# Query turns of the second head group in a list of their own, side work between the steps of norms, and the output product of eight heads inside the last attention

## The chip, the core and the metric

The kernel runs on one core of a Trainium2 chip. The metric is the device time of one execution in microseconds (us). Engines are named as in the profile: PE (TensorE, matmuls and transposes), DVE (VectorE), ACT (ScalarE), POOL (GpSimd) and SP (whose queue issues most DMAs). Every engine works through its own list of instructions in the order in which the list was written; between engines only semaphores order the work.

## The reference

Two decoder layers over x of 1024 tokens by 1024 channels, all in float32. Each layer is a token mixer and a feed-forward network, and each of these is preceded by an RMS norm with a shift and scale from a conditioning vector and followed by a gated residual sum:

```
for i in range(2):
    h = rmsnorm(x) * (1 + sc1) + sh1
    y = rglru_mixer(h) if i == 0 else dsa_mixer(h)
    x = x + g1 * y
    h = rmsnorm(x) * (1 + sc2) + sh2
    x = x + g2 * (square(relu(h @ w1)) @ w2)
```

Layer 0's mixer is a gated linear recurrence; the change does not touch that layer. Layer 1's mixer is a sparse attention: `h @ w_in` gives 16 query heads of 64, one key and value that all heads share, and 8 small indexer heads. The indexer's scores choose 256 keys for each query (a top-k by bisection); the queries attend to those alone; the 16 heads' results, 1024 channels, are multiplied by `w_out`.

## The kernel before

**Tiling.** Tokens are split into two halves (h = 0, 1) of 512, each of four blocks of 128 (t = 0 to 3 and 4 to 7). x lies with channels on partitions: eight tiles of 128 x 512 for each half. Weights come in by DMA as `raw`, are rounded by ACT into `wh` (L322) and the rest `raw - wh` goes into `wl` (L325, on POOL or DVE by the small list `self.lo`); a product is three matmuls `wh*hi`, `wh*lo`, `wl*hi` (L337 to L339).

**Order.** The Python code emits operations into a scheduler that fixes each engine's list at build time. Tiles come from pools with few slots: an instruction that needs a new tile waits until the last reader of the slot's former tile is done. Side work is held in Python generators: `self.bg` is a background whose steps `mix()` puts between main steps at `self.rate` steps each, and `self.fill` holds small steps (indexer heads, top-k) that `pump()` takes one by one.

**Layer 1 in time order.** (1) q, k, v and indexer projections of half 0, attention of half 0 (from 1378 us), its output product. (2) norm f1 of half 0 (L1396 to L1398): `stat` sums the squares by matmuls with ones (L71) and DVE and POOL take the root (L74, L76), DVE makes a diagonal (L79); `bc` broadcasts it by a matmul (L84); `apply` scales x (L102 to L104). (3) feed-forward of half 0. (4) projections and attention of half 1 (2012 to 2189 us), (5) its output product (two groups of eight heads, 96 matmuls each), (6) norm f1 of half 1, store of half 0's result, feed-forward of half 1, store of half 1.

**Queries.** `q_group` projects eight heads (group g) for four blocks, normalizes and rotates them, and appends for each block one list entry with two turns to `turns`: transposes on PE (`turn4`, L827) of two tiles that DVE and POOL write (L818, L819). A unit of attention that needs a turned query takes entries from the front of `turns` until it has its own.

**Attention.** A unit is (g, t, p): four heads of one query block; the 16 units of a half go through group 0 first. For each head: scores on PE (L1071, L1072), mask and row maximum on DVE (L1083), exponential on ACT (L1089), reciprocal of the sum on DVE (L1092), division of the whole row on POOL (L1094). Then per block of keys four heads' rows are transposed on PE (L1099), copied and rounded by ACT (L1101) and DVE (L1102), and multiplied by the values (L1111, L1112). A finished unit's result is split for the output product by ACT and POOL (L1126, 128 x 128). In half 1 the score rows `s` lie in the 13 slots that weights also use (`wh`, `wl`, `raw`). In this text heads of half 1 are counted from 0 to 63 and units from 0 to 15; unit k uses heads 4k to 4k+3, so units 8 to 15 are group 1.

The code around the change, with the order in which the parts are called:

```
self.bg, self.rate = F.f2_steps([F.NP - 2, F.NP - 1], 0), 0.8
self.attention(1, before)
self.finish()
self.reload(1)
run(self.proj_out(1, mod[1, 2], 0))
run(self.proj_out(1, mod[1, 2], 1, sqs("f1")))
```

## Time and profile before

| what | value |
|---|---|
| three runs | 2615.67, 2618.05, 2620.52 us; median 2618.05 |
| profiled execution | 2617.35 us, of which the span in the trace 2615.6 |
| PE busy | 2427.1 us, 93% of the span |
| DVE, ACT, POOL busy | 59%, 47%, 38% |
| matmuls and transposes on PE | 10834 |

The table is for the whole program. In single stages it reads differently: PE stands or runs at its lower clock for short stretches in layer 1, and in the attention of half 1 POOL has no idle time. The rows for that stand further down. In rows of the waits and of timelines "[7.28 <-POOL a L819]" means that the engine stood 7.28 us before this instruction, and that what ended last was POOL's line 819, which wrote the tile `a`. The granted clock (PEclk) is 1.00 for TensorE's upper level and 0.50 for its lower one.

### The profile page before, as it was taken

The numbers are of one execution on the slowest core, as the hardware profiler recorded it, in microseconds if no ns is written. First come the engines' busy times: TensorE is split into PE (matmuls) and PEld (weight loads), VectorE is DVE, ScalarE is ACT, GpSimd is POOL, SyncE is SP. The second block draws the span as 40 slices with busy tenths as digits, with TensorE's granted clock in tenths as the row PEclk, the third lists the DMA queues.
The fourth block names the chain that finished last, engine by engine and source line by source line (L and its number), as shares of the span: only waits on it lengthen the run. The fifth ranks groups of instructions, "written<-read, shape, count | busy, mean of one in ns | idle before, by whom it ended". The sixth has DMA issues, their size and how long they took to land. (4 is left out here: it accounts for less than half of the span.)

```text
span 2615.6 us, 30703 instructions
## 1 busy us (share of the span) xinstructions
PE 2427.1 (93%) x10834; PEld 1948.6 (74%) x10834; DVE 1546.9 (59%) x2873; ACT 1231.0 (47%) x2158; POOL 996.4 (38%) x584
## 2 busy tenths in 40 slices
PE   5689899898999999999996998999998998999999
PEld 3567678676788888888776876888887786788887
DVE  8677775579934421376686875575579894421212
ACT  3466463541122143235535767768753884433322
POOL 3454411222121244230136932223235996444342
PEclk7899999999999999999998998999999999999999
DMA  8677656326611278754431212223240003322231
GB/s 241 243 251 248 211 208 238 123 81 216 202 49 49 97 250 292 276 174 163 145 99 27 96 51 73 84 82 101 82 137 9 1 9 121 113 89 97 89 102 60
DMA packets 202748, 345.14 MB, mean 132 GB/s; under 512 B 19594, under 2 KB 109410, under 8 KB 202594
## 3 DMA queue, kind: packets, MB, share of 16 engines
q1 hardware_dynamic: 173648, 297.91, 33.6%
q10 hardware_dynamic: 28946, 45.27, 5.2%
q8 instruction: 85, 1.39, 0.2%
q14 instruction: 69, 0.57, 0.1%
HBM read 270.77 MB, written 72.35 MB: 131 GB/s over the span
## 5 line engine op out<-in xcount | busy, mean ns | idle before, releaser
L325 POOL TENSOR_TENSOR wl<-raw,wh 128x1024 fp32r<-128x1024 f32 (+2 forms) x242 | 597.1, 2476 | 1175.1 <-ACT wh L322 1128.2
L322 ACT CAST wh<-raw 128x1024 fp32r<-128x1024 f32 (+2 forms) x275 | 282.7, 1031 | 594.6 <-PE ps L338 270.7
L337 PE MATMUL ps<-a,wh 128*128 128x512 f32 x1152 | 462.5, 404 | 41.1 <-DVE a L682 13.9
L338 PE MATMUL ps<-a,wh 128*128 128x512 f32 x1152 | 461.4, 401 | 3.7 <-POOL a L664 2.2
L339 PE MATMUL ps<-a,wl 128*128 128x512 f32 x1152 | 459.4, 399 | 0.0
L337 PE MATMUL pd<-a,wh 128*128 128x512 f32 x1072 | 429.1, 401 | 21.6 <-DVE xc L595 13.8
L338 PE MATMUL pd<-a,wh 128*128 128x512 f32 x1072 | 428.0, 399 | 7.1 <-DVE a L100 5.7
L339 PE MATMUL pd<-a,wl 128*128 128x512 f32 x1072 | 427.2, 399 | 0.0
L174 DVE SCALAR_TENSOR_TENSOR a<-ps,mod,a 128x512 f32<-128x512 f32 x352 | 260.1, 745 | 264.2 <-PE ps L339 263.5
L337 PEld LDWEIGHTS ps<-a,wh 128*128 128x128 f32 x1152 | 220.0, 191 | 100.8 <-DVE a L682 16.0
L338 PEld LDWEIGHTS ps<-a,wh 128*128 128x128 f32 x1152 | 219.7, 191 | 57.9 <-POOL a L664 4.0
L339 PEld LDWEIGHTS ps<-a,wl 128*128 128x128 f32 x1152 | 219.2, 190 | 53.5
L337 PEld LDWEIGHTS pd<-a,wh 128*128 128x128 f32 x1072 | 202.4, 189 | 74.0 <-issue 14.5
L338 PEld LDWEIGHTS pd<-a,wh 128*128 128x128 f32 x1072 | 203.1, 189 | 59.8 <-DVE a L100 8.2
L339 PEld LDWEIGHTS pd<-a,wl 128*128 128x128 f32 x1072 | 203.1, 189 | 49.1
L1094 POOL TENSOR_SCALAR s<-s,rr 128x128 f32<-128x128 f32 (+7 forms) x128 | 224.9, 1789 | 22.3 <-DVE rr L1092 22.3
L337 PE MATMUL ps<-hid,wh 128*128 128x512 f32 x512 | 204.6, 400 | 12.9 <-DVE a L174 12.9
L978 ACT ACTIVATE signs<-sc,tc 128x384 int8<-128x384 f32 (+5 forms) x186 | 164.1, 882 | 92.9 <-DVE tc L993 79.4
L339 PE MATMUL ps<-hid,wl 128*128 128x512 f32 x512 | 204.0, 398 | 0.0
L338 PE MATMUL ps<-hid,wh 128*128 128x512 f32 x512 | 204.0, 398 | 0.0
L435 DVE SCALAR_TENSOR_TENSOR a<-a,cond,a 128x512 f32<-128x512 f32 x140 | 132.0, 974 | 45.0 <-DMA a<-in_ada_w_dram 44.3
L337 PEld LDWEIGHTS ps<-hid,wh 128*128 128x128 f32 x512 | 97.2, 190 | 39.4 <-DVE a L174 15.2
(270 smaller groups left out, 3715.9 us busy)
## 6 DMA issues: line engine op xcount, KB each, us to landing
raw<-in_ffn_w_dram SPq DMA_DIRECT2D x192, 512.0 KB, 3.6
a<-in_ada_w_dram ACTq DMA_DIRECT2D x160, 256.0 KB, 3.7
part<-wh SPq DMA_DIRECT2D x61, 512.0 KB, 3.6
part<-wl SPq DMA_DIRECT2D x61, 512.0 KB, 3.0
wh<-part SPq DMA_DIRECT2D x61, 512.0 KB, 3.3
wl<-part SPq DMA_DIRECT2D x61, 512.0 KB, 4.5
raw<-in_a_w_in_dram SPq DMA_DIRECT2D x20, 512.0 KB, 6.4
st<-in_ada_w_dram SPq DMA_DIRECT2D x32, 256.0 KB, 4.2
```

Of the source, the lines that this page charges most:

```text
L174: nc.vector.scalar_tensor_tensor(xt, ps, self.g2[:, m:m + 1], xt, op0=OP.mult, op1=OP.add)
L322: nc.scalar.copy(wh, raw)
L325: eng.tensor_tensor(wl, raw, wh.bitcast(FT), op=OP.subtract)
L337: pe.matmul(out, wh, xh, start=start, stop=False)
L338: pe.matmul(out, wh, xl, start=False, stop=False)
L339: pe.matmul(out, wl, xh, start=False, stop=stop)
L435: nc.vector.scalar_tensor_tensor(a, r, s, a, op0=OP.mult, op1=OP.add)
L978: A.activation(self.signs[:, 0:L], sc, AF.Sign, bias=0.0 if neg is None else neg.bitcast(FT), accum_out=n)
L1094: G.tensor_scalar(sl[e][:, 0:L], sl[e][:, 0:L], r[:, e:e + 1], None, op0=OP.mult)
```

## The change

- **Late turns.** `q_group` gets the list to append to. Group 1's entries go into `late_turns`; attention takes one entry of it after each unit from the second on, or when a unit of group 1 needs one.
- **Indexer heads in the norm of half 0.** Of the 16 head steps of blocks 6 and 7, four come ahead of `stat`, four between `stat` and `bc`, three after `apply`. The other five stay in `fill`.
- **Output product inside attention.** The first three steps of the feed-forward's background come ahead of the attention of half 1. When its rest is through and 12 units are done, x of half 1 is reloaded and group 0's output product runs in the background at 0.45 steps for each main step.
- **Stores.** Half 0's store (eight steps of four transposes, a copy and a DMA) is put around `stat` and `bc` of half 1's norm. Half of half 1's store (four steps, channels 0 to 511) is put behind the fifth to eighth output tile of the last feed-forward.

```diff
-    def q_group(self, h, g, hx):
+    def q_group(self, h, g, hx, turns):
...
-            self.turns.append([lambda p=p, turn=turn: turn(p) for p in range(2)])
+            turns.append([lambda p=p, turn=turn: turn(p) for p in range(2)])
...
+        def late():
+            for f in self.late_turns.pop(0):
+                f()
...
             while u not in self.turned:
-                if self.turns:
+                if g and self.late_turns:
+                    late()
+                elif self.turns:
                     self.turn_next()
...
             self.units = k + 1
+            if k and self.late_turns:
+                late()
             self.pump()
...
+            heads = self.idx_steps(6) + self.idx_steps(7)
+            some(4)
             N["f1", 0].stat()
+            some(4)
             N["f1", 0].bc()
             hf[0] = N["f1", 0].apply(mod[1, 4], mod[1, 3])
-            for t in (6, 7):
-                self.fill += self.idx_steps(t) + [lambda t=t: self.fill.extend(self.topk_steps(t))]
+            some(3)
+            self.fill += heads + self.topk_steps(6) + self.topk_steps(7)
...
-            self.bg, self.rate = F.f2_steps([F.NP - 2, F.NP - 1], 0), 0.8
+            f2 = F.f2_steps([F.NP - 2, F.NP - 1], 0)
+            for _ in range(3):
+                next(f2)
+            def background():
+                yield from f2
+                while self.units < 12:
+                    yield
+                self.reload(1)
+                self.rate = 0.45
+                yield from self.proj_out(1, mod[1, 2], 0)
+            self.bg, self.rate = background(), 0.8
             self.attention(1, before)
             self.finish()
-            self.reload(1)
-            run(self.proj_out(1, mod[1, 2], 0))
             run(self.proj_out(1, mod[1, 2], 1, sqs("f1")))
+            out0 = self.store(0, 0)
+            out0 += self.store(0, 1)
+            for f in out0[:3]:
+                f()
             N["f1", 1].stat()
+            for f in out0[3:6]:
+                f()
             N["f1", 1].bc()
             hf[1] = N["f1", 1].apply(mod[1, 4], mod[1, 3])
-            self.store(0)
-            FFN(self, 1, mod[1, 5], hf).single(1)
-            self.store(1)
+            for f in out0[6:]:
+                f()
+            early = self.store(1, 0)
+            def last(h, m):
+                if m >= 4:
+                    early.pop(0)()
+            FFN(self, 1, mod[1, 5], hf, last).single(1)
+            for f in self.store(1, 1):
+                f()
```

Three places in the engines' lists, of before and of the change. The first is PE's list at the start of half 0's attention: `ps<-identR,a` are the turns (L827), `ps<-ident,s` the transposes of score rows, `wh` and `wl` with 128 x 328 the key and value projection. Before:

```order
5300 L1072 MATMUL ps_11055<-a_8197,a_10235 128x384
5301 L827 MATMUL ps_11097<-identR,a_10782 128x128 x4
5302 L827 MATMUL ps_11103<-identR,a_10785 128x128 x4
5303 L827 MATMUL ps_11109<-identR,a_10796 128x128 x4
5304 L827 MATMUL ps_11115<-identR,a_10799 128x128 x4
5305 L827 MATMUL ps_11121<-identR,a_10810 128x128 x4
5306 L827 MATMUL ps_11127<-identR,a_10813 128x128 x4
5307 L1099 MATMUL ps_11133<-ident,s_10857 128x128 x4
5308 L778 MATMUL ps_11142<-wh_10887,a_10609 128x328
```

The same place in the changed kernel:

```order
5301 L1105 MATMUL ps_11097<-ident,s_10857 128x128 x4
5302 L778 MATMUL ps_11106<-wh_10887,a_10609 128x328
5303 L779 MATMUL ps_11106<-wl_10888,a_10609 128x328
5304 L780 MATMUL ps_11106<-wh_10887,a_10610 128x328
5305 L1105 MATMUL ps_11110<-ident,s_10940 128x128 x4
5306 L778 MATMUL ps_11106<-wh_10887,a_10627 128x328
5307 L779 MATMUL ps_11106<-wl_10888,a_10627 128x328
5308 L780 MATMUL ps_11106<-wh_10887,a_10628 128x328
5309 L827 MATMUL ps_11122<-identR,a_10782 128x128 x4
```

Six groups of four turns stood in front of the first score transposes; now these and six projection matmuls come first, the first two groups follow among the projection, and the other four later.

The second place is DVE's list at norm f1 of half 0, where `sc<-ir,wi,sc` (L954) adds an indexer head to the scores, L63 adds a square to the norm's sum, and L74, L79 and L102 belong to `stat` and `apply`. Before:

```order
1757 L63 TENSOR_TENSOR nl_12729<-nl_12729,ns_13063 128x512
1758 L954 SCALAR_TENSOR_TENSOR sc_12888<-ir_13070,wi,sc_12888 128x512
1759 L954 SCALAR_TENSOR_TENSOR sc_12888<-ir_13075,wi,sc_12888 128x256
1760 L74 TENSOR_SCALAR rs_13086<-ps_13081 128x4
1761 L991 TENSOR_SCALAR tl_13214<-tn_13215 128x1
1762 L993 TENSOR_SCALAR tc_13218<-tl_13214,tc_13060 128x1
1763 L79 TENSOR_SCALAR nl_13090<-ident,rs_13088 128x128 x4
1764 L991 TENSOR_SCALAR tl_13220<-tn_13221 128x1
```

In the changed kernel:

```order
1757 L63 TENSOR_TENSOR nl_12729<-nl_12729,ns_13063 128x512
1758 L993 TENSOR_SCALAR tc_13060<-tl_13056,tc_13036 128x1
1759 L954 SCALAR_TENSOR_TENSOR sc_12888<-ir_13070,wi,sc_12888 128x512
1760 L954 SCALAR_TENSOR_TENSOR sc_12888<-ir_13075,wi,sc_12888 128x256
1761 L950 TENSOR_SCALAR sc_13081<-ps_13083,wi 128x384
1762 L954 SCALAR_TENSOR_TENSOR sc_13081<-ir_13094,wi,sc_13081 128x512
1763 L954 SCALAR_TENSOR_TENSOR sc_13081<-ir_13099,wi,sc_13081 128x384
1764 L954 SCALAR_TENSOR_TENSOR sc_13081<-ir_13106,wi,sc_13081 128x512
1765 L954 SCALAR_TENSOR_TENSOR sc_13081<-ir_13111,wi,sc_13081 128x384
1766 L954 SCALAR_TENSOR_TENSOR sc_13081<-ir_13118,wi,sc_13081 128x512
1767 L954 SCALAR_TENSOR_TENSOR sc_13081<-ir_13123,wi,sc_13081 128x384
1768 L74 TENSOR_SCALAR rs_13131<-ps_13126 128x4
```

Between the last L63 and L74 stand now four heads' adds more, and seven adds between L79 and the first L102.

The third place is POOL's list in the last quarter of half 1's attention, where 128 x 1024 and 128 x 896 with `s<-s,rr` are the divisions of one head each. Before:

```order
476 L1094 TENSOR_SCALAR s_18811<-s_18811,rr_18815 128x1024
477 L1094 TENSOR_SCALAR s_18847<-s_18847,rr_18851 128x1024
478 L1094 TENSOR_SCALAR s_18882<-s_18882,rr_18886 128x1024
479 L1094 TENSOR_SCALAR s_18917<-s_18917,rr_18921 128x1024
480 L1094 TENSOR_SCALAR s_18944<-s_18944,rr_18948 128x1024
481 L325 TENSOR_TENSOR wl_19244<-raw_19241,wh_19243 128x1024
482 L1094 TENSOR_SCALAR s_18980<-s_18980,rr_18984 128x1024
```

In the changed kernel, from head 56 on:

```order
470 L1100 TENSOR_SCALAR s_18742<-s_18742,rr_18746 128x1024
471 L325 TENSOR_TENSOR wl_18788<-raw_18785,wh_18787 128x1024
472 L1132 TENSOR_TENSOR a_16956<-a_18673,a_16955 128x128
473 L1132 TENSOR_TENSOR a_16958<-a_18673,a_16957 128x128
474 L1132 TENSOR_TENSOR a_16960<-a_18673,a_16959 128x128
475 L1132 TENSOR_TENSOR a_16962<-a_18673,a_16961 128x128
476 L325 TENSOR_TENSOR wl_18794<-raw_18791,wh_18793 128x1024
477 L1100 TENSOR_SCALAR s_18809<-s_18809,rr_18813 128x1024
478 L1100 TENSOR_SCALAR s_18846<-s_18846,rr_18850 128x1024
479 L1100 TENSOR_SCALAR s_18893<-s_18893,rr_18897 128x1024
480 L1100 TENSOR_SCALAR s_18934<-s_18934,rr_18938 128x1024
481 L1100 TENSOR_SCALAR s_18977<-s_18977,rr_18981 128x1024
```

Another `wl` and then the last two divisions follow, so three splits of weights stand ahead of the last head's division where one stood. PE's list there, in unit 12, has the first matmuls of the output product between transposes of this unit's score rows:

```order
8546 L337 MATMUL ps_18797<-a_16947,wh_18787 128x512
8547 L338 MATMUL ps_18797<-a_16948,wh_18787 128x512
8548 L1105 MATMUL ps_18819<-ident,s_18491 128x128
8549 L1105 MATMUL ps_18819<-ident,s_18526 128x128
8550 L1105 MATMUL ps_18819<-ident,s_18560 128x128
8551 L1105 MATMUL ps_18819<-ident,s_18596 128x128
8552 L1105 MATMUL ps_18856<-ident,s_18491 128x128
8553 L339 MATMUL ps_18797<-a_16947,wl_18788 128x512
8554 L337 MATMUL ps_18797<-a_16949,wh_18787 128x512
```

Row 8553 reads the `wl` that POOL writes in its row 471; before, these matmuls stood behind the whole attention.

## Rows read from the trace of the kernel before

**Rows 1.** The engines over the whole span, from the page.

```profile
PE 2427.1 (93%) x10834; PEld 1948.6 (74%) x10834; DVE 1546.9 (59%) x2873; ACT 1231.0 (47%) x2158; POOL 996.4 (38%) x584
```

**Rows 2.** What PE waited for from 1370 us: total, times, longest, us.

```profile
PE ps L827 <- POOL a L819: 13.9, 5, 7.3
PE ps L1099 <- POOL s L1094: 11.2, 7, 4.3
PE ps L71 <- DVE nl L63: 8.9, 2, 6.2
```

**Rows 3.** PE's timeline, start of half 0's attention: start, length, instruction, idle before.

```profile
1387.50 0.34 PE L1072 MATMUL ps<-a,a 128*128 128x384 f32 x1
1395.11 0.75 PE L827 MATMUL ps<-identR,a 128*128 128x128 f32 x4 [7.28 <-POOL a L819]
```

**Rows 4.** Windows: length; busy (count) of PE, PEld, DVE, ACT, POOL; clock; DMA.

```profile
1390.00:1400.00 10.00, 2.25 (x12) 1.69 (x12) 10.00 (x31) 3.11 (x10) 9.52 (x10) 0.57 0.00 0
1400.00:1410.00 10.00, 4.58 (x21) 3.88 (x22) 4.24 (x14) 1.29 (x3) 9.06 (x11) 0.50 0.20 45
```

**Rows 5.** DVE's timeline in the same stretch.

```profile
1402.28 0.87 DVE L766 TENSOR_TENSOR q<-q,a 128x512 f32<-128x512 f32 x1
1407.73 0.69 DVE L1102 TENSOR_TENSOR pl<-ps,nl 128x512 fp32r<-128x512 f32 x1 [4.58 <-ACT nl L1101]
```

**Rows 6.** PE's timeline at norm f1 of half 0.

```profile
1575.08 1.87 PE L71 MATMUL ps<-ones,nl 128*128 128x1 f32 x8 [6.18 <-DVE nl L63]
1581.40 2.05 PE L84 MATMUL ps<-nl,ones 128*128 128x512 f32 x2 [4.45 <-DVE tl L991]
```

**Rows 7.** DVE's timeline there.

```profile
1578.31 2.94 DVE L79 TENSOR_SCALAR nl<-ident,rs 128x128 f32<-128x128 f32 x4 [0.85 <-POOL rs L76]
1583.48 2.06 DVE L102 SCALAR_TENSOR_TENSOR ns<-a,mod,ps 128x512 f32<-128x512 f32 x3 [1.92 <-PE ps L84]
```

**Rows 8.** Lines by shape, DVE, 1380 to 2010: an indexer head's adds.

```profile
L954 DVE SCALAR_TENSOR_TENSOR sc<-ir,wi,sc 128x512 f32<-128x512 f32 x35 | 30.8, 899 | 6.0 <-ACT ir L953 5.7
L954 DVE SCALAR_TENSOR_TENSOR sc<-ir,wi,sc 128x384 f32<-128x384 f32 x7 | 4.3, 610 | 0.0
```

**Rows 9.** Windows in half 1's attention and the product after it.

```profile
2120.00:2140.00 20.00, 19.49 (x116) 15.88 (x116) 18.23 (x40) 18.36 (x39) 20.00 (x13) 1.00 0.00 1
2160.00:2180.00 20.00, 12.75 (x63) 9.75 (x62) 7.96 (x15) 10.17 (x19) 20.00 (x12) 0.83 0.23 79
2180.00:2200.00 20.00, 19.95 (x93) 15.50 (x92) 9.65 (x14) 10.11 (x19) 11.21 (x9) 0.92 0.59 210
2200.00:2220.00 20.00, 20.00 (x88) 16.05 (x87) 5.95 (x8) 4.45 (x6) 9.54 (x4) 1.00 0.34 106
```

**Rows 10.** POOL's timeline, heads 51 to 63.

```profile
2139.20 18.27 POOL L1094 TENSOR_SCALAR s<-s,rr 128x896 f32<-128x896 f32 x7
2157.35 1.81 POOL L1126 TENSOR_TENSOR a<-a,a 128x128 fp32r<-128x128 f32 x4
2159.05 14.23 POOL L1094 TENSOR_SCALAR s<-s,rr 128x1024 f32<-128x1024 f32 x5
2173.15 2.44 POOL L325 TENSOR_TENSOR wl<-raw,wh 128x1024 fp32r<-128x1024 f32 x1
2175.48 2.94 POOL L1094 TENSOR_SCALAR s<-s,rr 128x1024 f32<-128x1024 f32 x1
```

**Rows 11.** PE's timeline: unit 15's start, last product, norm of half 1.

```profile
2178.47 0.47 PE L1099 MATMUL ps<-ident,s 128*128 128x128 f32 x1 [4.33 <-POOL s L1094]
...
2233.74 0.40 PE L339 MATMUL ps<-a,wl 128*128 128x512 f32 x1
2236.83 1.05 PE L71 MATMUL ps<-ones,nl 128*128 128x1 f32 x8 [2.69 <-DVE nl L63]
```

**Rows 12.** Timeline of all engines, end of the program.

```profile
2606.06 3.85 PE L1193 MATMUL ps<-ident,a 128*128 128x128 f32 x32
```

**Rows 13.** DMA issues, from the page: count, KB, us from issue to landing.

```profile
raw<-in_ffn_w_dram SPq DMA_DIRECT2D x192, 512.0 KB, 3.6
```

More of the change, by code (lines that the diff above doesn't have):

```diff
@@ L1185, in reload, with store, step @@
             self.nc.sync.dma_start(self.x[h, m], self.xd[h, m])
-    def store(self, h):
+    def store(self, h, c):
         nc = self.nc
-        for t in range(4):
-            for c in range(2):
-                ps = self.ps()
-                for b in range(4):
-                    nc.tensor.transpose(ps[:, b * P:(b + 1) * P], self.x[h, 4 * c + b][:, t * P:(t + 1) * P],
-                                        self.ident)
-                o = self.tmp("o")
-                (nc.scalar.copy if (t + c) % 2 else nc.vector.tensor_copy)(o, ps)
-                r = h * 4 + t
-                (nc.scalar if h == 0 else nc.sync).dma_start(
-                    self.out[0, r * P:(r + 1) * P, c * 512:(c + 1) * 512], o)
+        def step(t):
+            ps = self.ps()
+            for b in range(4):
+                nc.tensor.transpose(ps[:, b * P:(b + 1) * P], self.x[h, 4 * c + b][:, t * P:(t + 1) * P], self.ident)
+            o = self.tmp("o")
+            (nc.scalar.copy if (t + c) % 2 else nc.vector.tensor_copy)(o, ps)
+            r = h * 4 + t
+            (nc.scalar if h == 0 else nc.sync).dma_start(self.out[0, r * P:(r + 1) * P, c * 512:(c + 1) * 512], o)
+        return [lambda t=t: step(t) for t in range(4)]
     def run(self):
@@ L1241, in flush @@
                 turn_next()
-        self.turns, self.turn_next, self.turned = turns, turn_next, set()
+        self.turns, self.turn_next, self.turned, self.late_turns = turns, turn_next, set(), []
         NJ = 8
@@ L1339, in run @@
                       lambda: (idx(2), idx(3)), lambda: None, lambda: None, lambda: None,
-                      lambda: (flush(), run(self.q_group(0, 0, hm[0])))]
+                      lambda: (flush(), run(self.q_group(0, 0, hm[0], turns)))]
             for p in range(NJ, F.NP):
@@ L1354, in run @@
             self.lo = [1, 1, 0]
-            q1 = self.q_group(0, 1, hm[0])
+            q1 = self.q_group(0, 1, hm[0], self.late_turns)
             hm[1] = []
@@ L1391, in run, with some @@
                 heads.pop(0)()
+            heads = self.idx_steps(6) + self.idx_steps(7)
+            def some(n):
+                for _ in range(n):
+                    heads.pop(0)()
+            some(4)
             N["f1", 0].stat()
+            some(4)
             N["f1", 0].bc()
             hf[0] = N["f1", 0].apply(mod[1, 4], mod[1, 3])
-            for t in (6, 7):
-                self.fill += self.idx_steps(t) + [lambda t=t: self.fill.extend(self.topk_steps(t))]
+            some(3)
+            self.fill += heads + self.topk_steps(6) + self.topk_steps(7)
             self.lo, self.npump = [1, 1, 0], 2
@@ L1403, in run @@
             self.lo = [1, 0]
-            run(self.q_group(1, 0, hm[2]))
-            run(self.q_group(1, 1, hm[2]))
+            run(self.q_group(1, 0, hm[2], turns))
+            run(self.q_group(1, 1, hm[2], self.late_turns))
             self.lo = [1]
```

## The prediction, made before the changed kernel ran

> **What bounds the kernel now.** I read the page's engine line, then the view of waits for PE over layer 1, then windows and timelines of the four places that the diff names. The engine line says that PE is busy 93% of the span [rows 1]; the change takes no matmul away, so all it can win is PE's idle time and time at the lower clock, and only where PE's next work is not held by another engine. The view of waits names the holders from 1370 us: turns that wait for POOL's rotation (13.9 us), score transposes that wait for POOL's division (11.2) and the two norms' sums that wait for DVE (8.9) [rows 2]. The reader is to see that these three lie in three stages with different limits.
>
> At the start of half 0's attention PE ends its scores at 1387.50 and stands until 1395.11 for the first turn [rows 3]; in the next 20 us it works 2.25 and 4.58 us, at a granted clock of 0.57 and 0.50, while DVE is full until 1400 and POOL until 1410 [rows 4]. In half 1's attention POOL works 20.00 us of 20 [rows 9]: the divisions of the heads follow one another without a gap, and PE is in step with them. Unit 15's first transpose starts at 2178.47, after 4.33 us of waiting for POOL [rows 11], and POOL's last division began at 2175.48 [rows 10]. After the attention it is the other way round: PE 20.00 of 20, POOL 9.54 [rows 9].
>
> **Late turns in half 0: −8 us.** Six groups of turns leave the place ahead of the first score transposes. Two of the six (block 0 of group 1) come soon after and still wait for POOL until 1395, but now 8 transposes and 6 projection matmuls are done by then, and the rest of the 24 projection matmuls between and behind them. What is late next is DVE: its list up to the rotation that starts at 1402.28 and takes 0.87 is the same in both kernels, and the first rounding of transposed scores (L1102) stands behind it. There DVE idles 4.58 us before, since ACT's copy, and PE's transposes, stand behind the turns [rows 5]; now the roundings can run at 1403.2. The first costs 4.58 less. Behind it DVE works 4.39 of the ten us to 1420, so about as much again can be won until DVE's and POOL's own work (9 us of 10 in POOL's windows until 1410) closes in: 3 us at least, 14 at most (PE's idle time in 1390 to 1410, 7.75 + 5.42 = 13.2, and something for the clock), and I take 8, nearer to what DVE shows. The four groups that go on to later units are 16 transposes, under 2 us, which were executed before as well.
>
> **Heads in the norm of half 0: −2.5 us.** PE stands 6.18 us before `stat` and 4.45 before `bc` [rows 6]. Eleven heads are 44 matmuls; eight heads with two of 512 columns (0.23 us each, 20.00 for 88 [rows 9]) and two of 384 (0.17 by columns), three with four of 512, are 8 x 0.80 + 3 x 0.92 = 9.2 us of PE work that leaves the feed-forward behind. Against it: in DVE's list four heads' adds stand between the last square and L74. Their first is one instruction of 0.6 us, the others 3 x (0.90 + 0.61) = 4.5 [rows 8], so the root, the diagonal and `bc` come 5 us later. Between the diagonal and the first scaling stand seven adds, 3 x 0.90 + 4 x 0.61 = 5.1 us, of which the 2.2 us from the diagonal's end (1581.25) to 1583.48 are covered [rows 7]: 2.9 late. The scaling starts some 7 to 8 us later than at 1583.48 and PE's feed-forward with it; 9.2 less 7 is 2.2, and a little of the lower clock is gained. Ends: +2 if the lower clock stays as long as the longer wait, −8 if the heads' adds hide between DVE's other work. I take −2.5.
>
> **Stores: −2.5 us together.** At half 1's norm 24 transposes in place of standing time save 24 x 3.85 / 32 = 2.9 us [rows 12]; two copies on DVE stand ahead of the last square, 0.7 us lost: −2. At the end 16 transposes in place of 32 and four copies fewer save about 2.3 us, but the other 16 now stand in the feed-forward, where PE has no idle time, and cost 1.9: −0.5. The DMAs are issued from the lists of ACT and SP as before. Ends −4 and 0.
>
> **Output product of group 0 in the attention: +11 us.** The intent: 96 matmuls of 0.23 us, 22 us, go to where PE waits. What there is to fill: in 2160 to 2180 PE idles 7.25 us, and at clocks of 0.83 and 0.92 it loses 0.17 x 12.75 + 0.08 x 19.95 = 3.8 in the two windows [rows 9]: 11 us, the end of the range on this side (the stretches before have 0 to 2.5 of 20, in small pieces).
>
> But the product brings its weights' split along, and it stands in POOL's list, on the engine that is full. I count from the end of head 51's division, t0. Seven heads take 2139.20 to 2157.35; with four more of the first five's kind it is 5 x 2.50 + 2 x 2.82, so t0 = 2141.7, when unit 12 starts. Four splits of results take 1.7, a head of 1024 columns 2.82, a `wl` 2.33 (2173.15 to 2175.48) [rows 10].
> - POOL now: heads 52 to 55, 10.0; head 56, to 12.8; first `wl`, to 15.2.
> - PE now: two matmuls with `wh` and five transposes into unit 12 it meets the first matmul with `wl`. It gets there at about 4.4, when the weights' load (3.6 us [rows 13]), issued near the end of unit 11, and ACT's rounding are through, and stands until 15.2: **10.8 us, with the rest of unit 12 behind it**. In the kernel before PE did not stand there.
> - POOL next: the second `wl` waits for its load, which takes the place of the first one's `raw`, and for a slot that unit 12's transposes free: about 26. The `s` tiles of heads 57 and 58 need such slots too: head 57 from 28, heads 58 and 59 to 36.5. Heads 60 and 61 take the slots of the first `wh` and `wl`, whose last reader is late in unit 13: 42.7 to 48.3; third `wl` 50.7, heads 62 and 63 to 56.3. Before, head 63 ended at 36.6 (2175.48 + 2.82 − 2141.7).
> - PE to the end: unit 12 ends at 28, unit 13 at 43, unit 14 waits some 3 us for the third `wl`, unit 15 2 us for the fourth; with 89 matmuls of the product inside, the attention ends near 77. The other 103, at 0.23, end at 101, and 2 us for the lower clock behind the 10.8 us make 103. Before, the last matmul ended at 2234.1 [rows 11], at 92.4.
>
> The difference is 10.6; I take +11. It is +3 if POOL comes to the first `wl` a few heads earlier than its place says, and +20 if each of the four `wl` holds PE as the first one does. The three steps of the feed-forward ahead of the attention fill waits of PE before it, but POOL's chain starts when DVE's rotations are done, and those keep their order: 0, between −2 and +1.
>
> On this a page bears. In these rows one stage is full on POOL and the next on PE. The Trainium skill, "Perfetto Trace Analysis", section "Optimization Strategy", says that where the most-contended engine changes over time, interleaving such regimes may help. By it the term would be −11 instead of +11. I don't follow it, since the row of `wl` shows that the piece moved is not of PE alone.
>
> **The sum.** −8 − 2.5 − 2.5 + 11 = −2 against the profiled 2617.35 us (span 2615.6 and 1.75 around it). The median of the runs is 0.7 above that, so 2616. A measurement of this kernel can't tell a change within 0.2% (5.2 us) from none.
>
> **Rivals.**
> 1. *The product fills PE's waits.* POOL comes to the first `wl` in time, or PE's standing there is covered. For it: 11 us of losses at the end of the attention, and a POOL with 9.54 of 20 behind it. Against: the row in POOL's list behind head 56. Price: −8 − 2.5 − 2.5 − 11 = −24, so 2594; half of it, with a term of 0, 2605.
> 2. *Slower: the lower clock behind the stall.* After the 7.28 us of standing at 1387 the clock was 0.50 to 0.57 for 20 us [rows 3, 4], with little work in them; unit 12 to 14 are dense work. A matmul costs double at the lower of the two levels; 20 us of it do 10 us of full work. Price +10 on the sum, so 2626, and with further stands for `wl` 2631. It decides from some 7 us of loss by the clock on. The Trainium skill, "TensorE: Matmul & The Clock Gate", "Part 1: The HAM clock gate", says that the throttled state is the default and activity releases it; that rule is for this rival, and by it the time is the one given here.
> 3. *Late turns win nothing.* POOL works 9.52 and 9.06 of 10 until 1410 [rows 4], and what it does there is the same; if the divisions of the next units wait behind its rotations, PE only waits elsewhere. Price: 8 us back, 2624.
> 4. *It doesn't do what it says.* The background might not reach the product before the units are over; then the term is 0: 2605. The list shows 89 matmuls inside, which speaks against it.
>
> **How the numbers follow.** My forecast, 2612 to 2623 when the parts cancel: 0.34. Rival 1 with its half and rival 4: 0.37, nearly all faster. Rival 2: 0.19. Rival 3 and the like: 0.10. So faster 0.37, no difference 0.34, slower 0.29. The range leaves out the full price of rival 1 and the far end of rival 2: 2598 to 2632; the forecast's own is 2611 to 2623.
>
> **What would show it.** In the new trace: PE standing about 11 us in unit 12 before L339, released by POOL's L325; POOL with two gaps of some 6 us in the attention's last quarter; the last division 15 to 20 us later against unit 12's start; PE's wait at 1387 down from 7.28 to pieces; `stat` of half 0 with heads before it and L74 5 us later. Wrong I am if PE's idle time in the attention's last quarter shrinks, or if 1387 to 1424 loses as much as before.

## The result and the profile after

The changed kernel takes 2630.66 us (median of 5 runs, 2627.64 to 2634.67) against 2618.05 for the kernel before on the same chip. The ratio is 1.0051, with a 95% interval of 1.0039 to 1.0064: 12.6 us slower. The forecast was 2616, no difference, from a sum of -2 over the steps of the change.

To find where the time went I cut both traces at the same instructions and compared how long each piece took. The pieces come from single profiled executions; the stretch ahead of the first piece (layer 0 and the first projections), which the change leaves as it was, differs by 2.6 us between the two, so a piece under some 2 us is not read as a gain or a loss by itself. The profiled execution of the changed kernel took 2634.42 us, 3.8 above its median. All pieces run from the start of one instruction to the start of the next one named.

| piece | before, us | change, us | forecast |
|---|---|---|---|
| first scores of half 0 to `stat` (attention, its product) | 195.5 | -1.8 | late turns -8 |
| `stat` to first matmul of the feed-forward | 9.9 | +6.1 | heads: +7 |
| that to the last projection matmul of half 1 | 395.9 | -11.1 | heads: -9.2 |
| that to the first score transpose of half 1 | 41.7 | +4.2 | three steps: 0 |
| that to the division of head 51 | 116.6 | +0.5 | 0 |
| that to the division of head 63 | 36.3 | +22.5 | product: |
| that to the last matmul of the product | 58.2 | -4.6 | +11 with the row above |
| from there to the end | 381.9 | -1.3 | stores: -2.5 |

The engines over the whole span, to be held against [rows 1]: PE's busy time is up by 13.3 us with the same 10834 instructions. A matmul that runs at the lower clock is busy for longer (the fence on unit 12 below has 0.80 us for one that takes 0.40 elsewhere). Most of it is no work of the change: 8.3 us lie ahead of half 0's attention, where PE is busy 1260.9 us before and 1269.3 now for the same 5390 instructions.

```profile
PE 2440.4 (93%) x10834; PEld 1958.1 (74%) x10834; DVE 1531.6 (58%) x2873; ACT 1231.3 (47%) x2158; POOL 995.3 (38%) x584
```

What PE waited for from 1370 us on (total, times, longest, us), to be held against [rows 2]:

```profile
PE ps L339 <- POOL wl L325: 13.8, 4, 9.0
PE ps L827 <- DVE a L174: 10.9, 1, 10.9
PE ps L1105 <- POOL s L1100: 7.6, 8, 2.2
PE ps L778 <- DVE mn L1089: 5.7, 1, 5.7
PE ps L1077 <- DVE mn L1089: 5.3, 2, 3.1
PE ps L1105 <- DVE pl L1108: 4.2, 3, 2.2
PE ps L84 <- DVE nl L79: 4.1, 2, 2.6
```

Of the three leaders of before only the divisions are left (7.6 us for 11.2); the turns' wait for POOL and the norms' wait for L63 have shrunk to 0.3 and 1.4 us. In their places stand two new releasers with 24.7 us together, a weight split on POOL and an addition on DVE (L174). Both belong to what was moved into or ahead of half 1's attention.

**The product inside the attention.** POOL's timeline from head 49 on; 128 x 1024 and 128 x 896 on L1100 are divisions of a head, L325 the splits of weights. Before, it was a chain without a gap [rows 10].

```profile
2137.19 17.88 POOL L1100 TENSOR_SCALAR s<-s,rr 128x896 f32<-128x896 f32 x7
2155.00 2.37 POOL L325 TENSOR_TENSOR wl<-raw,wh 128x1024 fp32r<-128x1024 f32 x1
...
2168.04 2.37 POOL L325 TENSOR_TENSOR wl<-raw,wh 128x1024 fp32r<-128x1024 f32 x1 [9.01 <-PE ps L1105]
2172.69 8.49 POOL L1100 TENSOR_SCALAR s<-s,rr 128x1024 f32<-128x1024 f32 x3 [2.28 <-PE pd L1078]
2187.68 5.67 POOL L1100 TENSOR_SCALAR s<-s,rr 128x1024 f32<-128x1024 f32 x2 [6.51 <-DVE rr L1098]
2193.32 2.35 POOL L325 TENSOR_TENSOR wl<-raw,wh 128x1024 fp32r<-128x1024 f32 x1
2195.66 5.66 POOL L1100 TENSOR_SCALAR s<-s,rr 128x1024 f32<-128x1024 f32 x2
```

The engine that had no idle time now stands 9.01, 2.28 and 6.51 us. PE's timeline in unit 12 says why, and then the end of the product:

```profile
2147.10 0.50 PE L337 MATMUL ps<-a,wh 128*128 128x512 f32 x1 [1.74 <-ACT wh L322]
...
2147.67 0.71 PE L1105 MATMUL ps<-ident,s 128*128 128x128 f32 x5
2157.42 0.80 PE L339 MATMUL ps<-a,wl 128*128 128x512 f32 x1 [9.05 <-POOL wl L325]
...
2227.36 0.80 PE L338 MATMUL ps<-a,wh 128*128 128x512 f32 x1 [2.76 <-POOL a L1132]
```

PE stands until POOL, behind heads 52 to 56, has made the first `wl`; POOL then stands until PE, late by that, has released slots for the second one (its wait of 9.01 us ends with a transpose of score rows, L1105). Each waits for the other in turn. The windows show it for both, and what the clock did (columns as in [rows 4], to be held against [rows 9]):

```profile
2140.50:2160.50 20.00, 7.42 (x29) 5.64 (x30) 3.75 (x8) 5.48 (x13) 18.52 (x11) 0.77 0.14 49
2160.50:2180.50 20.00, 18.18 (x90) 14.00 (x89) 11.40 (x20) 9.88 (x17) 10.19 (x4) 0.97 0.08 28
2180.50:2200.50 20.00, 16.02 (x77) 12.29 (x77) 12.29 (x23) 12.08 (x24) 13.49 (x6) 0.91 0.16 53
```

One window over the whole stretch, from the end of head 51's division to the product's last matmul, tells how much of the loss is standing and how much is the clock. First before, then changed:

```profile
2141.80:2234.15 92.35, 85.03 (x404) 67.33 (x402) 49.34 (x82) 47.98 (x84) 64.46 (x36) 0.94 0.31 103
2142.24:2252.50 110.26, 88.67 (x403) 69.02 (x404) 48.54 (x78) 48.31 (x83) 64.17 (x37) 0.91 0.19 63
```

PE stands 21.6 us in place of 7.3, which is 14.3 of the 17.9 us; its busy time for the same matmuls is 3.6 us longer, at a mean granted clock of 0.91 in place of 0.94.

**The start of half 1's attention.** PE's timeline, and then DVE's of the same moment:

```profile
1985.58 0.40 PE L339 MATMUL ps<-a,wl 128*128 128x512 f32 x1
1996.92 1.23 PE L827 MATMUL ps<-identR,a 128*128 128x128 f32 x8 [10.94 <-DVE a L174]
```

```profile
1995.43 0.69 DVE L766 TENSOR_TENSOR q<-q,a 128x512 f32<-128x512 f32 x1
1996.03 0.75 DVE L174 SCALAR_TENSOR_TENSOR a<-ps,mod,a 128x512 f32<-128x512 f32 x1
1996.69 0.49 DVE L818 CAST a<-q 128x256 fp32r<-128x256 f32 x2
```

The three early steps of the feed-forward run on PE until 1985.6. A matmul's result lies in a bank of PSUM, and the bank can be written anew when another engine has read it. The banks that the three steps filled are emptied by L174, and in DVE's list the last of these stands among the rotations of queries. The next turn needs a bank, so it waits 10.94 us for a DVE instruction that is in no hurry. Before, PE's larger waits in this place were two, of 6.6 us together:

```profile
1986.01 1.26 PE L827 MATMUL ps<-identR,a 128*128 128x128 f32 x8 [4.26 <-ACT q L908]
...
2000.36 0.50 PE L337 MATMUL ps<-a,wh 128*128 128x512 f32 x1 [2.37 <-DVE a L174]
```

**The norm of half 0.** PE, DVE and POOL, to be held against [rows 6, 7]:

```profile
1575.90 1.70 PE L71 MATMUL ps<-ones,nl 128*128 128x1 f32 x8
1585.33 2.04 PE L84 MATMUL ps<-nl,ones 128*128 128x512 f32 x2 [2.55 <-DVE nl L79]
```

```profile
1580.21 0.15 DVE L74 TENSOR_SCALAR rs<-ps 128x4 f32<-128x4 f32 x1
1584.31 0.88 DVE L79 TENSOR_SCALAR nl<-ident,rs 128x128 f32<-128x128 f32 x4 [3.29 <-POOL rs L76]
1589.20 2.06 DVE L102 SCALAR_TENSOR_TENSOR ns<-a,mod,ps 128x512 f32<-128x512 f32 x3
```

```profile
1580.32 2.96 POOL L325 TENSOR_TENSOR wl<-raw,wh 128x1024 fp32r<-128x1024 f32 x1 [3.75 <-ACT wh L322]
1583.24 1.04 POOL L76 TENSOR_TENSOR rs<-rs,mhalf 128x4 f32<-128x4 f32 x1
```

The wait before `stat` is gone and the one before `bc` is 2.55 instead of 4.45. The scaling starts 13.3 us after `stat` where it took 8.4 before. Of the 4.9 us that this is later, 2.4 are the heads' adds ahead of L74 (4.3 us after `stat`; it was 1.9). From L74 to the diagonal it is 2.8 us longer, and that is on POOL: the root (L76) now stands behind a split of weights, 2.96 us long, that began 0.11 us after L74. The rest nearly cancels: the diagonal is done in 0.88 us where it took 2.94 [rows 7], and the seven adds behind it put the scaling off by 1.8.

**Late turns.** PE at the start of half 0's attention, then the windows, 2.6 us later than those of [rows 4] because the attention starts so much later; then DVE:

```profile
1390.30 0.60 PE L1105 MATMUL ps<-ident,s 128*128 128x128 f32 x4
1396.55 0.64 PE L778 MATMUL ps<-wh,a 128*128 128x328 f32 x1 [5.65 <-DVE mn L1089]
```

```profile
1392.60:1402.60 10.00, 6.05 (x31) 5.41 (x32) 10.00 (x31) 3.59 (x11) 9.52 (x10) 0.66 0.00 0
1402.60:1412.60 10.00, 6.43 (x31) 4.80 (x29) 8.69 (x27) 3.87 (x13) 10.00 (x13) 0.74 0.24 53
1412.60:1422.60 10.00, 5.92 (x19) 4.63 (x19) 4.93 (x17) 4.20 (x10) 5.59 (x8) 0.50 0.00 1
```

```profile
1404.94 0.87 DVE L766 TENSOR_TENSOR q<-q,a 128x512 f32<-128x512 f32 x1
1405.73 0.68 DVE L1108 TENSOR_TENSOR pl<-ps,nl 128x512 fp32r<-128x512 f32 x1
...
1415.78 0.26 DVE L856 TENSOR_SCALAR kk<-kk,ss 128x64 f32<-128x64 f32 x1 [2.91 <-POOL ss L855]
```

DVE's hole of 4.58 us [rows 5] is filled, the rounding follows the last rotation at once, as forecast. But the wait of 7.28 us [rows 3] is only moved: the first matmul of the projection stands 5.65 us, now for a bank that DVE's row maximum (L1089) has to read first, and that stands in DVE's list behind rotations. And the third window, in which PE did 33 matmuls at a clock of 0.84 before, has 19 at 0.50.

**Stores.** The last transposes, against [rows 12]: a run of 20 is left, and the program ends 2.3 us sooner after the feed-forward's last matmul.

```profile
2625.48 2.54 PE L1202 MATMUL ps<-ident,a 128*128 128x128 f32 x20
```

### The profile page after: what moved, and what is told of

Same layout as the page of the kernel before. It is cut to its first block, busy times and chain, and to the rows that moved or that the text cites. A ratio compares the mean times of both kernels' runs of the same rounds, so it can differ in the third digit from the quotient of the medians.

```text
span 2632.6 us, 30717 instructions
## 1 busy us (share of the span) xinstructions
PE 2440.4 (93%) x10834; PEld 1958.1 (74%) x10834; DVE 1531.6 (58%) x2873; ACT 1231.3 (47%) x2158; POOL 995.3 (38%) x584
## 5 line engine op out<-in xcount | busy, mean ns | idle before, releaser
L325 POOL TENSOR_TENSOR wl<-raw,wh 128x1024 fp32r<-128x1024 f32 (+2 forms) x242 | 596.9, 2474 | 1183.3 <-ACT wh L322 1141.2
L174 DVE SCALAR_TENSOR_TENSOR a<-ps,mod,a 128x512 f32<-128x512 f32 x352 | 260.5, 747 | 271.8 <-PE ps L339 271.0
L339 PEld LDWEIGHTS ps<-a,wl 128*128 128x128 f32 x1152 | 219.8, 191 | 68.5 <-POOL wl L325 15.2
L337 PEld LDWEIGHTS pd<-a,wh 128*128 128x128 f32 x1072 | 203.3, 190 | 72.4 <-issue 13.3
L1100 POOL TENSOR_SCALAR s<-s,rr 128x128 f32<-128x128 f32 (+7 forms) x128 | 225.0, 1777 | 34.9 <-DVE rr L1098 31.7
L152 DVE TENSOR_TENSOR a<-r,a 128x512 fp32r<-128x512 f32 x64 | 47.3, 761 | 139.4 <-ACT a L151 138.1
```

The costliest lines, as they stand in the source:

```text
L152: nc.any.tensor_tensor(ql, r, qh.bitcast(FT), op=OP.subtract)
L174: nc.vector.scalar_tensor_tensor(xt, ps, self.g2[:, m:m + 1], xt, op0=OP.mult, op1=OP.add)
L325: eng.tensor_tensor(wl, raw, wh.bitcast(FT), op=OP.subtract)
L337: pe.matmul(out, wh, xh, start=start, stop=False)
L339: pe.matmul(out, wl, xh, start=False, stop=stop)
L1100: G.tensor_scalar(sl[e][:, 0:L], sl[e][:, 0:L], r[:, e:e + 1], None, op0=OP.mult)
```

## The experiments

The kernel before ran again in each batch (medians 2618.0 to 2621.8), so I compare ratios to it; 0.001 is 2.6 us.

**Which of the two pieces at half 1 costs.** Without the product inside, without the three steps, and without either:

```diff
# e1_no_product (and e3)
-                while self.units < 12:
-                    yield
-                self.reload(1)
-                self.rate = 0.45
-                yield from self.proj_out(1, mod[1, 2], 0)
...
+            self.reload(1)
+            run(self.proj_out(1, mod[1, 2], 0))
# e2_no_three (and e3)
-            for _ in range(3):
-                next(f2)
```

> The changed kernel with group 0's output product put back behind the attention of half 1; all else as changed. Theory P (the product inside the attention costs 17 to 18 us, because its weights' splits stand in POOL's full list and hold PE): 2630.7 less 17.6, about 2613. Rival F (the three feed-forward steps ahead of the attention are the main cost, by the 11 us for which PE then waits for DVE): the product's removal gives little, about 2627.

> The changed kernel without the three feed-forward steps ahead of the attention of half 1; the product stays inside. Theory P: the three steps cost only the 4.2 us of lead that PE has at the last query projection and has lost when the first score transposes start, so about 2626.5, and PE's stand of 9 us in unit 12 stays. Rival F: about 2619.

> The changed kernel with both undone: the product behind the attention and no feed-forward steps ahead of it. Left are late turns, indexer heads and stores. If the parts add up: 2630.7 - 17.6 - 4.2 = 2609, that is 9 us faster than before. If late turns in half 1 also cost something, 2612 to 2616.

Measured: e1 2613.57, ratio 0.9984 (0.9975 to 0.9993); e2 2627.79, 1.0036 (1.0023 to 1.0050); e3 2608.20, 0.9963 (0.9951 to 0.9976). All three came as expected, within 1.5 us. In e1 the piece with heads 51 to 63 is 36.3 us long again, in e2 the piece before the first transpose is as before. So the product inside costs some 18 us (e3 to e2: 0.0073 x 2620 = 19) and the three steps some 5 (0.0021 x 2620 = 5.5); the rest of the change wins 9.7.

**What in the product costs.** Two suspects: POOL's split of the weights, and the slots that score rows and weights share. All these kernels are without the three early steps, except e4. In e4 and e12 DVE makes `wl` (from there on, so that of group 1's product too). In e5 and e6 the weights of half 1's product of group 0 stand in half-size tiles of another pool, so that a split of 128 x 1024 becomes two of 128 x 512, and group 1's weights are still split by POOL. So a row and a column of the table below differ by a little more than their heading says.

```diff
# e4_wl_dve, e12_dve_shared_slots
                 self.rate = 0.45
+                self.lo = [0]
# e5_own_slots_pool; in e6_own_slots_dve nc.vector in place of nc.gpsimd
+            raw = self.wp.tile([P, 2, 512], FT, name=self.nm("raw"), tag="raw", bufs=3)
+            self.nc.sync.dma_start(raw, src)
+            for e in range(2):
+                wh, wl = self.tileR(), self.tileR()
+                self.nc.scalar.copy(wh, raw[:, e])
+                self.nc.gpsimd.tensor_tensor(wl, raw[:, e], wh.bitcast(FT), op=OP.subtract)
```

> The changed kernel with the product's weights split by DVE in place of POOL. Theory P1 (their place in POOL's list is the cost): PE's stand of 9 us for the first one goes, POOL loses four splits (9.4 us), the last division comes some 10 us earlier against unit 12's start; 2616 to 2620. Rival P2 (slots: the product's weights take six of the 13 slots that score rows need, so divisions wait for transposes, whoever splits): POOL's two gaps of 9.0 and 6.5 us before heads 57 and 60 stay, PE's stand only moves; 2626 to 2630.

> As e2 (product inside the attention, no early feed-forward steps), but the product's wh and wl lie in eight tiles of the activations' pool, so that only raw takes slots of the score rows; POOL still splits. Theory P1 (POOL's list) : PE's stand of 7 to 9 us in unit 12 stays, the gaps of POOL before heads 57 and 60 shrink, in all 3 to 6 us less than e2's 2627.8: 2622 to 2625. Theory P2 (slots): both gaps go and with them most of the loss, 2612 to 2616.

> As e5, with DVE as the splitter. If place in POOL's list and slots were the whole of what kept the product from filling PE's waits, it should now give what the page's rule promises: up to 11 us less than e3's 2608.2, so 2598 to 2604. If PE had nothing to win there (its waits are given back to the unit that comes later), 2607 to 2612. DVE works 18 of 20 us there, so it may become the holder: 2612 to 2616.

> e6 with the product's weights back in the 13 slots that they share with score rows, DVE as the splitter (that is e4 without the early feed-forward steps). If slots and splitter are two separate costs: e4's 2615.5 less 4, 2611, that is 7 us more than e6. If DVE's splitting alone is what counts, 2604 to 2606.

| ratio to before | split on POOL | split on DVE |
|---|---|---|
| shared slots | e2 1.0036 (1.0023 to 1.0050) | e12 0.9965 (0.9953 to 0.9977) |
| own slots | e5 1.0002 (0.9994 to 1.0011) | e6 0.9944 (0.9931 to 0.9958) |
| product not inside | e3 0.9963 (0.9951 to 0.9976) | |

e4 gave 2615.50 (0.9992, 0.9981 to 1.0002), e5 2620.66, e6 2604.12, e12 2612.79. e5 lies between the two theories; e4 and e6 lie at the edge of the first range that each named, and e12, 5.5 us behind e6 by the ratios, is nearer to two separate costs than to one. Splitting on DVE is worth 18.6 us with shared slots and 15 with own ones; own slots 9 and 5.5. The traces have the same order: from the end of head 51's division to the product's last matmul it is 92.3 us before, 110.0 in e2, 102.5 in e5, 95.5 in e12 and 85.1 in e6. Both costs are real, POOL's list is the larger. POOL's timeline in e4 shows the second one alone: no split is left on it, and it still stands twice (in e12, which has no early steps, 7.87 and 5.66 us).

```profile
2132.08 17.89 POOL L1100 TENSOR_SCALAR s<-s,rr 128x896 f32<-128x896 f32 x7
...
2159.24 8.49 POOL L1100 TENSOR_SCALAR s<-s,rr 128x1024 f32<-128x1024 f32 x3 [7.60 <-DVE rr L1098]
2173.41 12.38 POOL L1100 TENSOR_SCALAR s<-s,rr 128x1024 f32<-128x1024 f32 x4 [5.68 <-DVE rr L1098]
```

In e6 neither is left. POOL divides to the end without a gap, and PE's windows show the product in what were its waits:

```profile
2133.08 18.47 POOL L1100 TENSOR_SCALAR s<-s,rr 128x896 f32<-128x896 f32 x7
...
2151.88 2.93 POOL L1100 TENSOR_SCALAR s<-s,rr 128x1024 f32<-128x1024 f32 x1
...
2155.98 17.06 POOL L1100 TENSOR_SCALAR s<-s,rr 128x1024 f32<-128x1024 f32 x6
```

```profile
2154.50:2174.50 20.00, 19.70 (x109) 16.01 (x107) 17.22 (x30) 13.01 (x24) 18.54 (x10) 1.00 0.24 80
2174.50:2194.50 20.00, 19.51 (x110) 15.91 (x110) 12.22 (x20) 12.19 (x24) 8.82 (x7) 1.00 0.41 132
```

PE works 19.70 and 19.51 us of 20 at a granted clock of 1.00, where [rows 9] had 12.75 at 0.83. From the division of head 51 to the last matmul of the product it is 7.2 us less than before: in the trace a gain of the kind that rival 1 spoke of is there, but not to be had with this weight path. e6 is faster than both kernels, by 15 us against before. Against e3, which leaves the product outside, it is 5 us by the ratios, and the two intervals still overlap, so that the product inside wins anything at all rests on the trace.

**The parts alone**, each put into the kernel before:

```diff
# e7_late_only (cut)
-            q1 = self.q_group(0, 1, hm[0])
+            q1 = self.q_group(0, 1, hm[0], self.late_turns)
...
+            if k and self.late_turns:
+                late()
...
# e8_heads_only (cut)
+            some(4)
             N["f1", 0].stat()
+            some(4)
             N["f1", 0].bc()
...
# e11_stores_only (cut)
-            self.store(0)
...
+            out0 = self.store(0, 0)
...
```

> The kernel before with late turns alone, in both halves. The forecast's term was -8: 2610. The two traces show 2 to 3 us from 1378 us to the norm's statistics of half 0 and nothing at the first transposes of half 1: 2615 to 2616.

> The kernel before with the indexer heads between the norm's steps alone. The forecast's term was -2.5: 2615.5. The two traces show 4 to 5 us between the norm's statistics of half 0 and the query projection of half 1: 2613 to 2614.

> The kernel before with the stores moved alone. The forecast's term was -2.5; the stages of the traces so far give -1.2 from the norm of half 1 to the feed-forward, +1.3 within it and -2.3 at the end: 2618 less 2.2, 2616. If the parts' sum (e3, -9.8) lacks 5 us that late turns and heads alone don't show, they must be here: 2612.

Measured: e7 2617.96, 0.9993 (0.9984 to 1.0001); e8 2618.38, 0.9997 (0.9986 to 1.0008); e11 2619.18, 0.9993 (0.9982 to 1.0003). Each interval reaches to no change. By the ratios e7 and e11 are 1.8 us faster, in line with what was expected of the traces, and e8 0.8, where 4 to 5 were expected: a miss. Together the three win 0.0017 of the time, and e3, which has all three, wins 0.0037 (0.0024 to 0.0049): 5 us apart. In the traces the heads' pieces are in e8 as in e3 (+6.2 and -11.1), with 1.2 us lost in the piece before them, where four heads run ahead of `stat`; and late turns win 3.0 in half 0 in e7, so the -1.8 of the changed kernel is -3.0 and these +1.2; but the piece from head 63 to the end of the product is 1.0 to 1.7 us longer than before in each of the three, and 0.2 shorter in e3. Why is open; the margins of the four ratios allow most of it to be noise.

**Why late turns won 1.8 and not 8.** First the place of group 1's rotations: e9 (on e3) and e10 (on e6) put them behind the projection of keys and values inside the attention, e13 (on e3) ahead of it.

```diff
# e9_late_rotation, e10_best (e13_rotation_first: `yield from q1` as the first line of the background)
-            run(q1)
             self.drain()
...
                 yield from feed(self.kv_steps(1, hm[1]), 2)
+                yield from q1
```

> e3 (no product inside, no early feed-forward steps), and group 1's rotations of half 0 are done in the attention's background behind the projections of the second half's keys, not ahead of the attention. Theory R (late turns won 2 to 3 us in place of 8 because group 1's rotations still stand ahead on DVE and POOL: score reductions, and with them PE's banks, wait behind them): PE's stand of 5.6 us for DVE's reduction goes, half 0's norm starts 5 to 10 us earlier than e3's, 2598 to 2603. Rival S (POOL's divisions bind half 0's attention later on anyway): no earlier norm, 2607 to 2610.

> e6 (product inside, its weights in tiles of their own, split by DVE) with the late rotations of e9. If the two add up, e6's 2604.1 less what e9 gains on e3: 2594 to 2599 by theory R, 2603 to 2606 by rival S.

> The changed kernel without the product inside and without the three early steps (2608), and in the background of half 0's attention the rotations of group 1 stand first, ahead of the projection's roundings and norms. If the late turns won 1.8 us and not 8 because score roundings on DVE stand behind group 1's rotations at places that hold PE's PSUM banks (5.65 and 3.09 us of standing), then these stands go or move together and half 0's attention is some 5 us shorter: 2603. If POOL's list sets the stretch (its share of the rotations and the key norm's L855 at 1415.8 behind them), nothing changes: 2608.

Measured: e9 2630.41, 1.0032 (1.0021 to 1.0044); e10 2623.34, 1.0005 (0.9993 to 1.0017); e13 2622.56, 1.0002 (0.9993 to 1.0012). All three miss, on the slow side. In e9 the wait of 5.6 us is gone, and the largest waits of PE between 1375 and 1590 are now at the first units of group 1, which reach rotations that are late:

```profile
PE ps L1077 <- DVE mn L1089: 12.4, 2, 8.5
PE ps L827 <- POOL a L819: 9.8, 1, 9.8
```

Half 0's attention is 9.7 us longer than in e3, and half 1's 6.3 us (12.9 lost behind its first transpose, 6.6 won before it); that second loss I did not follow up. In e13 half 0 is 1.6 us longer and half 1 7.6. So the rotations are not simply in the way where they stand: moved either way, they cost more.

Then POOL's share: in e14 (on e3) ACT divides the score rows of the first two blocks, for the heads of group 0.

```diff
# e14_act_divides
-                G.tensor_scalar(sl[e][:, 0:L], sl[e][:, 0:L], r[:, e:e + 1], None, op0=OP.mult)
+                if t < 2 and g == 0:
+                    A.activation(sl[e][:, 0:L], sl[e][:, 0:L], AF.Copy, scale=r[:, e:e + 1])
+                else:
+                    G.tensor_scalar(sl[e][:, 0:L], sl[e][:, 0:L], r[:, e:e + 1], None, op0=OP.mult)
```

> The same kernel (2608) with the divisions of the first two blocks' scores in half 0's attention on ACT in place of POOL. If POOL's list sets the first 40 us of the attention, the key norm of group 1 (L856, at 1415.8) comes some 7 us earlier and half 0's attention ends some 5 us earlier: 2603. If DVE's list and the PSUM banks set it, L856 comes earlier but the attention's length stays: 2608. A loss of some us is possible if ACT, which copies and rounds in the same stretch, is then late for PE.

Measured: 2614.03, 0.9969 (0.9959 to 0.9980), no different from e3 (0.9963). The windows:

```profile
1390.00:1400.00 10.00, 3.56 (x20) 3.06 (x19) 10.00 (x31) 7.68 (x28) 2.53 (x3) 0.72 0.07 25
1400.00:1410.00 10.00, 8.96 (x46) 7.62 (x45) 9.52 (x32) 6.03 (x18) 6.23 (x7) 0.77 0.20 45
```

POOL works 2.53 and 6.23 of ten where it had nearly all, and DVE is as full as in the changed kernel (10.00 and 9.52 here, 10.00 and 8.69 there). The key norm (L856) comes 31.8 us after the attention's start instead of 33.6 in e3, and half 0's attention is 1.6 us shorter, while POOL has nearly 11 us less to do in these two windows. ACT took the work over (7.68 and 6.03 us of ten), so a loss there that hides a gain is not excluded, but ACT is not full. With that reservation the theory that POOL's list sets this stretch falls. DVE's list remains, nearly full for these 20 us in the changed kernel and in e14. No run made it shorter: that it is the limit is what is left over, not what was shown.

## Why the prediction was wrong

**The product inside: right mechanism, +17.9 where I had taken +11.** PE stood where it was said to and for what: 9.05 us plus 1.74 for `wh`, the first `wl` at +15.2 us after head 51's end, as worked out; the second `wl` at 25.8 against "about 26". From there POOL ran 2.3 to 2.8 us late (head 57 started at 30.5 and not 28, head 63 ended at 59.1 and not 56.3), and the attention on PE ended at 79.3, not 77. Behind the attention 103 matmuls took 30.6 us, not 24 + 2. There PE stands once more, 0.94 us for ACT and 2.76 us for POOL, which makes three weight splits (7.04 us) ahead of the last unit's results, and the next 13 matmuls start 0.43 us apart, at a clock of 0.66 in the windows there, instead of 0.23. The step that failed here is the end of the walk: the forecast followed POOL's list to the last division and not to its next consumer. The far end of the term, +20, held the result, but by luck: it was to come if each `wl` held PE as the first did, and the other three held it 4.8 us together.

**The three steps: 0, between -2 and +1, was wrong; +4.2 by the trace, 3.9 to 7.1 by the runs.** This is the step whose reason failed. I said that POOL's chain starts when DVE's rotations are done and those keep their order. They do, but PE's work ahead of the attention has another end on DVE: L174, which empties its PSUM bank. It stands among the rotations, and the turn behind it stood 10.94 us. The steps filled a wait of PE and made a longer one. That I costed them by PE and POOL alone, without asking who releases the bank, is the mistake. Three pairs of kernels show the cost: e1 against e3 5.5 us, the full change against e2 3.9, e4 against e12 7.1.

**Late turns: -8 was too much; -1.8, or -3.0 alone.** The filled hole in DVE's list was right, and what it was said to be worth "at least", 3 us, is what came. I took 8 as "nearer to what DVE shows". The step that failed is "8 transposes and 6 projection matmuls are done by then": by 1397.6, the same moment 2.6 us later, it was 4 and 3, because the first projection matmul stood 5.65 us for a bank that DVE frees behind rotations. It is the same omission as with the three steps. What closed in is named in the prediction, DVE's and POOL's own work, but its date was wrong: it closes in at once. PE did more in the two first windows (6.05 and 6.43 us against 2.25 and 4.58 [rows 4]), at granted clocks of 0.66 and 0.74, and then stood again. What would win the rest of the 8 us stays open. That this is rival 3's case, nearly, is true in size. Its reason (POOL) is not: e14 took most of POOL's work away and won 1.6.

**Heads: -5.0 where I had -2.5; -3.8 with the 1.2 us ahead of `stat` (e8).** Eleven heads took 11.1 us out of the feed-forward, not 9.2, and the start came 6.1 us later against some 7. The delay has another make-up than I worked out: 2.8 us of it are POOL's weight split ahead of the root. In the times it shows less than in the trace (e8).

**Stores: -1.3 in the full change, -2.2 without the three steps, against -2.5.** Right within what the runs can tell.

**The sum.** -1.8 - 5.0 + 4.7 + 17.9 - 1.3 = +14.5 by the traces, with +2.6 of the stretch ahead of the pieces the 17.0 between the two spans; +12.6 by the medians. Against the forecast of -2, 7 us come from the product, 5 from the three steps and 5 from the late turns (at -3.0); heads (at -3.8) and stores cancel. The time lies where rival 2 put it, but not for its reason: from head 51 to the product's end the lower clock took 3.6 us more of PE's busy time than before (88.67 against 85.03) and not 10, and 14.3 of the 17.9 us are standing. Rival 1's price, 22 us better than my term, was met by two thirds in e6's trace (the product 7.2 us better than before, against a price of 11), once both obstacles were gone. That a measurement can't tell a change within 0.2% was too careful: the margins came out at some 0.1%. On the rule of the Trainium skill that was weighed there ("Perfetto Trace Analysis", section "Optimization Strategy": where the most-contended engine changes over time, interleaving such regimes may help) the runs say both: +17.9 us as the change has it, -7.2 us with the split off the full engine and slots of its own. Rivals 2 and 3 had between them 0.29 for slower, and the errors of three terms, all to one side, decided.

## What to carry to other kernels

Before moving matmuls into a stretch where PE waits, list what each of them needs and what it holds: the split of its weights, the slot, the PSUM bank and the instruction that empties it, and look on which in-order list each of these lands. If one lands on the engine that the stretch waits for, the move costs a wait on both sides (here +18 us; with the split on another engine and slots of its own, -7, both by the traces). Follow the fuller engine's list past the stretch to its next consumer, and when a hole on one engine is filled, take the bound from the engine that is full on both sides of it.

## What the runs showed of the hardware beside this

The same difference of two tiles costs on POOL 2.35 to 2.37 us for 128 x 1024 (POOL's timeline of the changed kernel above) and 1.30 for 128 x 512 (mean of 8 in e5), on DVE 1.24 and 0.88 (means of 11 and 8 in e4 and e6). Two divisions of a score row of 128 x 256 took 2.02 us on POOL and 0.91 on ACT (e14). Which engine did the small side operation was worth more here than any of the moves, 15 to 18.6 us for the split, but not by its length alone: e14 halved the time of a division as well and won nothing. PE had stood 9.05 us for the split in unit 12, but only 0.3 us for divisions in half 0's attention of e3.
